# Two pairs of 512-column projections, from eight products to seven, in a two-layer encoder

## The chip, the core and the metric

The kernel is one program on one core of a Trainium2 chip. TensorE (PE) multiplies, VectorE (DVE), ScalarE (ACT) and GpSimd (POOL) do the elementwise work, and SyncE (SP) issues transfers. The metric is the device time of one execution in microseconds; lower is better.

## What is computed

Two layers on 512 tokens by 1024 channels, all float32. `u` is the RMS-normed input of a layer.

```python
proj = u @ w_in                                   # [512, 1024] @ [1024, 7424]
dq, dk, dv, rq, rk, rv, rg, gq, gk, gv, gates = split_cols(proj, IN_SPLITS)
a = differential_attention(rope(norm(dq)), rope(norm(dk)), dv, lam)      # 4 heads
r = silu(rg) * group_norm(bidirectional_retention(rope(rq), rope(rk), rv))  # 4 heads
c = grouped_query_attention(axial(norm(gq)), axial(norm(gk)), gv)        # 8 heads
merged = sum(sigmoid(gates) * (branches @ w_branch))                     # 3 branches
h = h + merged @ w_out
h = h + relu(rms_norm(h) @ w_mlp_in) ** 2 @ w_mlp_out
```

`c0` below means 256 columns of `dq` with 256 of `dk` (heads 0 and 1), `c1` the other 256 of each (heads 2 and 3).

## The kernel before

**Products.** TensorE's fast float32 (`fp32r`) takes a shortened number, so every operand is cut into a part `hi` and the rest `lo`. One product is then three matmuls: hi by hi, hi by lo, lo by hi. The weights come from memory in quarters of [128, 1024] through two `stage` buffers (SP's DMAs). ACT casts the quarter to `w_hi`, DVE subtracts it to give `w_lo` (line 417 records all of these operations, line 411 all matmuls). Six buffers hold the parts (`BUFS_W`).

**The mixing half of a layer** (`mix`) has a background and a side. The background (`bg`) is the stream of projections: `rv`; then for four heads `rq`, `rk`, `rg`; then `c0`, `dv`, `c1`, `gq`, each with tokens down the partitions (`units_b`: four token tiles, each of 8 k tiles by 3 matmuls of 512 columns); then `gkv`; then the merges of the three branches (`merge`), with gates and branch projections. The side is the attention: four retention heads (`ret_head`), four heads of the differential attention (`diff_head`), eight of the grouped one. `weave` puts `RATE` side steps beside each few passes of the background. A `diff_head` starts when all four token tiles of its `c` are there.

**Pairs in seven products.** Some gates (28 units in the program) and W1 of the MLP already use Winograd's form of Strassen's algorithm: two units of weights by two halves of tokens in seven products of half size in place of eight (`pair`). It needs sums of right operands; for the gates `turn_operands` makes them (lines with `xg`, `t`, `t23`, `t4`), in four steps within the merges (`TURN_AT`).

**What sets the order.** Every instruction is first noted (`Plan.note`), with a key in the order of the code. `Plan.order` then replays the program with a price for each instruction and lets each engine take the first ready one by key. What comes out is a fixed order for each engine: an engine that waits holds all that is behind it. So the diff shows little of how work moves, and the built order of each engine is shown with the change.

Buffers of [128, 512] come from one pool of 51 (`g`); PSUM has three banks for projections (`mm`), two for scores (`sc`), two for transposes (`tr`) and one for the sums of attention (`av`).

## Time and profile before

| | |
|---|---|
| runs shown | 1792.59 us median of 3, from 1791.82 to 1793.54 |
| span of the profiled execution | 1791.8 us, which is the time of the lowest run to 0.1 us |
| PE busy | 1767.7 us, 99% of the span, 10216 matmuls |
| DVE busy | 1376.4 us, 77% |
| ACT busy | 983.2 us, 55% |
| POOL busy | 297.1 us, 17% |
| granted TensorE clock | 1.000 (2.4 GHz) |
| transfers | 172.50 MB, 96 GB/s in the mean |

Busy shares are averages over stages. The record of a matmul or of a DVE operation is longer than the step to the next one, since the next begins before the last has drained: so what a stream of them costs is read from the starts in the timeline, not from the mean duration. `PE x <- DVE c` in the view of waits means that the matmul that writes `x` waited for the DVE operation that writes `c`.

### The profile page before, as it was taken

The numbers are of one execution on the slowest core, as the hardware profiler recorded it, in microseconds if no ns is written. First come the engines' busy times: TensorE is split into PE (matmuls) and PEld (weight loads), VectorE is DVE, ScalarE is ACT, GpSimd is POOL, SyncE is SP. The second block draws the span as 40 slices with busy tenths as digits, with TensorE's granted clock in tenths as the row PEclk, the third lists the DMA queues.
The fourth block names the chain that finished last, engine by engine and source line by source line (L and its number), as shares of the span: only waits on it lengthen the run. The fifth ranks groups of instructions, "written<-read, shape, count | busy, mean of one in ns | idle before, by whom it ended". The sixth has DMA issues, their size and how long they took to land.

```text
span 1791.8 us, 26264 instructions
## 1 busy us (share of the span) xinstructions
PE 1767.7 (99%) x10216; PEld 1544.8 (86%) x10216; DVE 1376.4 (77%) x2084; ACT 983.2 (55%) x1568; POOL 297.1 (17%) x294
## 2 busy tenths in 40 slices
PE   8999999999999999999999999999999999999999
PEld 6887888889989989999888778888888899989897
DVE  7866797899979766678656677968999797566783
ACT  5545666784446655445444455768844466444450
POOL 3334472002210000000013335700111100000000
PEclk9999999999999999999999999999999999999999
DMA  6311212112352323333432121121133423234331
GB/s 203 105 61 49 93 49 79 59 37 95 107 170 101 118 94 118 123 115 116 152 106 71 48 80 62 59 63 56 39 104 130 159 83 134 95 102 128 121 113 56
DMA packets 53691, 172.50 MB, mean 96 GB/s; under 512 B 6336, under 2 KB 6848, under 8 KB 53568
## 3 DMA queue, kind: packets, MB, share of 16 engines
q1 hardware_dynamic: 53568, 170.84, 29.4%
q8 instruction: 80, 1.31, 0.3%
q14 instruction: 43, 0.35, 0.1%
HBM read 162.43 MB, written 8.39 MB: 95 GB/s over the span
## 4 chain that ended last, share of the span: by engine, by line
PE 82%; DVE 8%; issue 3%; POOL 3%; ACT 2%; DMA 1%; SPq 0%; DVEq 0%; ACTq 0%; POOLq 0%
PE x L411 21%; PE w L411 20%; PE gate L411 6%; PE proj L411 5%; PE wo L411 5%; PE c L411 4%; PE wtr L413 2%; PE rv L411 2%; DVE w_lo L417 2%; PE rg L411 2%; PE rq L411 2%; PE dsc L411 2%; PE gav L411 2%; PE gsc L411 2%; DVE c L417 1%
## 5 line engine op out<-in xcount | busy, mean ns | idle before, releaser
L417 ACT CAST w_hi<-stage 128x1024 fp32r<-128x1024 f32 (+1 forms) x283 | 276.6, 982 | 319.7 <-PE w L411 120.7
L417 DVE TENSOR_TENSOR w_lo<-stage,w_hi 128x1024 fp32r<-128x1024 f32 (+1 forms) x283 | 336.9, 1192 | 78.7 <-ACT w_hi L417 75.8
L411 PE MATMUL x<-u,w_hi 128*128 128x256 f32 x1472 | 273.5, 284 | 5.3 <-DVE c L417 5.3
L411 PEld LDWEIGHTS x<-u,w_hi 128*128 128x128 f32 x1472 | 232.3, 192 | 10.9 <-DVE c L417 8.2
L411 PE MATMUL x<-u,w_lo 128*128 128x256 f32 x736 | 208.0, 283 | 0.0
L411 PE MATMUL w<-ml,w_hi 128*128 128x512 f32 (+1 forms) x520 | 200.3, 386 | 0.0
L411 PE MATMUL w<-mh,w_lo 128*128 128x512 f32 (+1 forms) x520 | 200.1, 386 | 0.0
L411 PE MATMUL w<-mh,w_hi 128*128 128x512 f32 (+1 forms) x520 | 200.1, 387 | 0.0
L411 PEld LDWEIGHTS x<-u,w_lo 128*128 128x128 f32 x736 | 141.1, 192 | 0.0
L417 ACT ACTIVATE c<-c 128x512 f32<-128x512 f32 x156 | 98.4, 631 | 32.9 <-DVE c L417 30.2
L411 PEld LDWEIGHTS w<-mh,w_lo 128*128 128x128 f32 x520 | 97.8, 188 | 19.5
L411 PEld LDWEIGHTS w<-ml,w_hi 128*128 128x128 f32 x520 | 97.8, 188 | 18.7
L411 PEld LDWEIGHTS w<-mh,w_hi 128*128 128x128 f32 x520 | 97.8, 188 | 18.5
L411 PE MATMUL gate<-u,w_hi 128*128 128x512 f32 x320 | 107.3, 399 | 0.0
L411 PE MATMUL x<-t23h,w_lo 128*128 128x256 f32 x368 | 104.2, 283 | 0.0
L411 PE MATMUL x<-t23l,w_hi 128*128 128x256 f32 x368 | 104.0, 283 | 0.0
L411 PE MATMUL x<-t23h,w_hi 128*128 128x256 f32 x368 | 103.9, 283 | 0.0
L417 ACT CAST w_hi<-sa 128x1024 fp32r<-128x1024 f32 x46 | 48.5, 1053 | 77.0 <-DVE sa L417 55.9
L411 PE MATMUL c<-w_hi,u 128*128 128x512 f32 x256 | 86.1, 394 | 0.0
L417 POOL TENSOR_TENSOR gth<-gth,c 128x512 f32<-128x512 f32 x28 | 45.9, 1647 | 179.0 <-DVE c L417 179.0
L417 DVE TENSOR_TENSOR c<-x,pu 128x512 f32<-128x512 f32 x92 | 63.1, 686 | 12.0 <-PE x L411 11.3
L411 PEld LDWEIGHTS x<-t23l,w_hi 128*128 128x128 f32 x368 | 70.6, 192 | 0.0
(278 smaller groups left out, 4554.5 us busy)
## 6 DMA issues: line engine op xcount, KB each, us to landing
stage<-in_w SPq DMA_DIRECT2D x283, 512.0 KB, 3.6
h<-in_x SPq DMA_DIRECT2D x16, 256.0 KB, 5.3
mid<-h SPq DMA_DIRECT2D x16, 256.0 KB, 2.0
h<-mid SPq DMA_DIRECT2D x16, 256.0 KB, 4.8
keep<-h SPq DMA_DIRECT2D x8, 256.0 KB, 4.1
h<-keep SPq DMA_DIRECT2D x8, 256.0 KB, 3.9
out<-h SPq DMA_DIRECT2D x7, 256.0 KB, 2.0
t_ret<-in_t_ret SPq DMA_DIRECT2D x4, 256.0 KB, 4.9
```

Of the source, the lines that this page charges most:

```text
L411: self.nc.tensor.matmul(k.pop("out"), **k)
L413: self.nc.tensor.transpose(k["out"], k["in_"], k["identity"])
L417: getattr(getattr(self.nc, o.engine), o.name)(**k)
```

## The change

`c0` with `dv`, and `c1` with `gq`, become two pairs in the seven-product form (`pair_wide`, keys `wa` and `wb`): A are 256-row halves of the two 512-column weights, B the token halves, and a product is [128 tokens, 512 columns] twice. Fourteen pieces of weights per pair are cut in place of eight quarters. The sums of weights (S1 to S4) are made by transfers: GpSimd issues a DMA that adds a quarter into the buffer `sa` or `sb`.

With it come: the right operands are made one step after each retention head, copied to memory and brought back in the merges, since they would fill the pool; the retention heads' results go to memory and back as well; `gkv` follows `rv`; `rq`, `rk`, `rg` of three heads and all branch weights are cut without DVE (`BY_DMA`): a GpSimd DMA casts to `w_hi`, ACT writes its negative to `w_lo`, a second GpSimd DMA adds the weight to it; prefetching goes by steps; `BUFS_W` is 5, `BUFS_G` 53, `RATE` 0.8; the Plan's price of a matmul is 11 ns higher.

```diff
+BY_DMA = {(nm, h) for nm in ("rq", "rk", "rg") for h in (1, 2, 3)} | {("br", n, i) for n in range(3) for i in range(4)}
+WIDE = ("A11", "A12", "S1", "S2", "S4", "S3", "A22")
+WIDE_PRODUCTS = (1, 2, 5, 6, 3, 7, 4)
-BUFS_W = 6
+BUFS_W = 5
-AHEAD_LOAD = 6
-AHEAD_SPLIT = 2
-BUFS_G = 51
-RATE = 1.0
+AHEAD = 2
+BUFS_G = 53
+RATE = 0.8
...
-            return 2.5 + n / 2.4 * (1 if n >= 256 else 4)
+            return 13.7 + n / 2.4 * (1 if n >= 256 else 4)
...
-        self.p_s = pool("s", 1)
+        self.p_s = pool("s", {"sa": 2, "sb": 1})
...
+    def cut_dma(self, q):
+        nc, n = self.nc, WIDTH[q % NQ]
+        hi, lo = (x[:, 0:n] for x in self.parts(self.p_w, 1024))
+        nc.gpsimd.dma_start(out=hi, in_=self.a["w"][q][:, 0:n])
+        nc.scalar.activation(out=lo, in_=hi, func=AF.Copy, scale=-1.0)
+        nc.gpsimd.dma_start(out=lo, in_=self.a["w"][q][:, 0:n], accum_op=ALU.add)
+        return hi, lo
...
+    def cut_wide(self, q, op, k):
...
+        if op[0] == "A":
+            return self.part(self.p_w, 1024, self.load(at(op)))
+        if op == "S1":
+            w[k] = self.load(at("A21"), self.p_s, "sa")
+        if op == "S3":
+            w[k] = self.load(at("A21"), self.p_s, "sb")
+        more(w[k], {"S1": "A22", "S2": "A11", "S3": "A11", "S4": "A12"}[op])
+        return self.part(self.p_w, 1024, w[k])
...
+    def pair_wide(self, l, key, u, n_cols, evs):
...
+        for o, n in enumerate(WIDE_PRODUCTS):
+            ps = [self.psum("mm", f"wide{n}")[:, 0:n_cols] for _ in range(2)]
+            for k in range(2):
...
+                for s in range(2):
+                    for j in (2 * k, 2 * k + 1):
+                        xh, xl = (self.right(u, n, p, j)[:, s * 128:(s + 1) * 128] for p in range(2))
+                        c = slice((j % 2) * n_cols, (j % 2 + 1) * n_cols)
+                        self.passes(ps[s], [(xh, hi[:, c]), (xh, lo[:, c]), (xl, hi[:, c])], j == 0, j == 3)
+                    yield
+            for s, p in enumerate(ps):
+                if n in (1, 5):
+                    copy(n, s, p)
+                elif n == 6:
+                    sub(kept[1, s], p, kept[1, s])
+                    sub(kept[5, s], kept[1, s], kept[5, s], ALU.add)
...
         def bg():
+            turn, uu = self.turn_operands(u), None
             yield from self.units_b(l, ("rv",), u, 512, 2, lambda p, t: self.ev_rv(p, t, st))
+            yield from self.units_b(l, ("gkv",), u, 256, 4, lambda p, t: self.ev_gkv(p, t, st))
             for h in range(4):
...
-            yield from self.units_b(l, ("c", 0), u, 512, 2, lambda p, t: self.ev_qk(p, 0, t, st))
-            yield from self.units_b(l, ("dv",), u, 512, 2, lambda p, t: self.ev_dv(p, t, st))
-            yield from self.units_b(l, ("c", 1), u, 512, 2, lambda p, t: self.ev_qk(p, 1, t, st))
-            turn, uu = self.turn_operands(u), None
+                uu = next(turn)
+            self.put_away(uu)
+            yield from self.pair_wide(l, ("wa",), uu, 512, [lambda x, t: self.ev_qk(x, 0, t, st),
+                                                            lambda x, t: self.ev_dv(x, t, st)])
+            back = self.bring_back(u)
...
-            yield from self.units_b(l, ("gq",), u, 512, 2, lambda p, t: self.ev_gq(p, t, st))
-            yield from self.units_b(l, ("gkv",), u, 256, 4, lambda p, t: self.ev_gkv(p, t, st))
-            yield from merge(1, True, False, "ret")
+            yield from merge(1, True, False, "ret", M1[0])
+            yield from self.pair_wide(l, ("wb",), uu, 512, [lambda x, t: self.ev_qk(x, 1, t, st),
+                                                            lambda x, t: self.ev_gq(x, t, st)])
+            yield ("after", "ret")
+            for h in range(4):
+                st["bT", 1, h] = (self.g("rTh", F32R), self.g("rTl", F32R))
+                for p, x in enumerate(st["bT", 1, h]):
+                    self.nc.sync.dma_start(out=x.bits(), in_=self.away["r", h, p])
+            yield from merge(1, True, False, "ret", M1[1])
```

**First place: DVE's queue where the heads of the differential attention meet the second projection of `q` and `k`.** (`qk<-c` and `qss` belong to the projection `c1`; `mx`, `drc`, `dE`, `dwl`, `dq` to differential heads; `w_lo` to cuts of weights.) Before, in `c1`:

```order
L417 TENSOR_TENSOR qk<-c,gqk 128x512
L417 RECIPROCAL drc<-dss 128x2
L417 TENSOR_REDUCE mx<-dsc 128x1
L417 TENSOR_TENSOR drc<-drc,lam 128x2
L417 TENSOR_REDUCE qss<-sq 128x8
L417 TENSOR_SCALAR qk_m<-qss,epst 128x8
L417 TENSOR_TENSOR dwl<-wtr,dwh 128x512
```

Now, in `wb` at its fourth product (`wide_2134` and `wide_2227` are that product's two PSUM banks, `p_...` the running sums in SBUF):

```order
L467 TENSOR_TENSOR w_lo<-sa,w_hi 128x1024
L467 TENSOR_TENSOR p_1994<-wide_2134,p_1994 128x512
L467 SCALAR_TENSOR_TENSOR dE_2141<-dE_2141,drc,dE_2178 128x512
L467 TENSOR_TENSOR p_2224<-p_1994,p_2224 128x512
L467 TENSOR_TENSOR w_lo<-sb,w_hi 128x1024
L467 TENSOR_TENSOR dwl<-wtr,dwh 128x512 x2
L467 TENSOR_TENSOR p_2001<-wide_2227,p_2001 128x512
L467 TENSOR_TENSOR w_lo<-stage,w_hi 128x1024
L467 TENSOR_TENSOR w_lo<-sa,w_hi 128x1024
L467 TENSOR_TENSOR dq<-qtr,dq 64x512 x2
```

The sums of the pair and the cuts of its pieces now stand between the steps of the heads.

**Second place: PE's queue in the same stretch.** (`u_...` are parts of x g; `t1h`, `t1l`, `t23h`, `t23l` parts of turned right operands; `dav` and `dsc` matmuls of a differential head.) Before, in `c1`:

```order
L411 MATMUL dav<-dwl,dvh 128x256
L411 MATMUL dav<-dwh,dvl 128x256
L411 MATMUL dav<-dwh,dvh 128x256
L411 MATMUL dav<-dwl,dvh 128x256
L411 MATMUL c<-w_hi,u_156 128x512
L411 MATMUL c<-w_lo,u_156 128x512
L411 MATMUL c<-w_hi,u_170 128x512
```

Now, at the change from the third product (`wide_2072`) to the fourth (`wide_2134`):

```order
L461 MATMUL wide_2072<-w_hi,t1h 128x512
L461 MATMUL wide_2072<-w_lo,t1h 128x512
L461 MATMUL wide_2072<-w_hi,t1l 128x512
L461 MATMUL wide_2134<-w_hi,t23h 128x512
L461 MATMUL dsc<-dkh,dq 128x512
L461 MATMUL dsc<-dkl,dq 128x512
L461 MATMUL wide_2134<-w_lo,t23h 128x512
L461 MATMUL wide_2134<-w_hi,t23l 128x512
```

A product's matmuls have the form of those of `c1`, three for each k tile, with the attention's between them; the left operands are turned ones.

**Third place: POOL's queue in the retention heads.** Before it held rotary work alone (`sw`, `rot`), the heads' factors (`msr`) and gates (`rx`):

```order
L417 TENSOR_TENSOR sw<-sw,t_ret 128x512
L417 TENSOR_TENSOR rot<-rot,sw 128x512
L417 TENSOR_TENSOR msr<-msq,mhalf 128x4
L417 TENSOR_TENSOR rx<-rx,rsg 128x512
L417 TENSOR_TENSOR sw<-sw,t_ret 128x512
```

Now the transfers that cast and add weights stand in it:

```order
L467 DMA w_hi<-in_w 128x1024
L467 DMA w_lo<-in_w 128x1024
L467 TENSOR_TENSOR msr<-msq,mhalf 128x4
L467 TENSOR_TENSOR sw<-sw,t_ret 128x512
L467 TENSOR_TENSOR rot<-rot,sw 128x512
L467 DMA w_lo<-in_w 128x1024
L467 DMA w_hi<-in_w 128x1024
L467 TENSOR_TENSOR rx<-rx,rsg 128x512
```

Each `w_lo` transfer waits for ACT, each `w_hi` transfer for PE to give back a buffer, and the rotary work behind them waits along.

## Rows read from the trace of the kernel before

**Rows 1.** The page, parts 1 and 2: busy time by engine; GB/s in 40 slices.

```profile
PE 1767.7 (99%) x10216; PEld 1544.8 (86%) x10216; DVE 1376.4 (77%) x2084; ACT 983.2 (55%) x1568; POOL 297.1 (17%) x294
...
GB/s 203 105 61 49 93 49 79 59 37 95 107 170 101 118 94 118 123 115 116 152 106 71 48 80 62 59 63 56 39 104 130 159 83 134 95 102 128 121 113 56
```

**Rows 2.** Busy time by stretch: mixing (180 to 300, 360 to 480), MLP (660 to 720).

```profile
core 0: us, PE busy (x) PEld busy (x) DVE busy (x) ACT busy (x) POOL busy (x), PEclk, DMA share, GB/s
180.00:240.00 60.00, 59.73 (x313) 48.99 (x312) 48.55 (x85) 37.90 (x73) 29.26 (x32) 1.00 0.21 66
240.00:300.00 60.00, 59.57 (x360) 51.77 (x359) 50.42 (x100) 39.61 (x80) 33.86 (x45) 1.00 0.24 82
360.00:420.00 60.00, 60.00 (x363) 52.74 (x363) 57.57 (x103) 45.07 (x84) 5.15 (x2) 1.00 0.17 52
420.00:480.00 60.00, 57.83 (x407) 53.72 (x406) 58.40 (x76) 26.23 (x34) 12.20 (x8) 1.00 0.29 99
660.00:720.00 60.00, 60.00 (x385) 54.81 (x384) 38.20 (x53) 29.41 (x40) 0.00 (x0) 1.00 0.33 106
```

**Rows 3.** Timeline of PE: start, duration, line, operation; 512, 256 and 128 columns.

```profile
699.81 0.39 PE L411 MATMUL w<-ml,w_hi 128*128 128x512 f32 x1
...
702.75 0.39 PE L411 MATMUL w<-mh,w_lo 128*128 128x512 f32 x1
...
252.11 0.28 PE L411 MATMUL dav<-dwh,dvl 128*128 128x256 f32 x1
252.23 0.28 PE L411 MATMUL dav<-dwh,dvh 128*128 128x256 f32 x1
...
183.73 1.03 PE L413 MATMUL wtr<-ident,dE 128*128 128x128 f32 x8
184.53 0.48 PE L411 MATMUL c<-w_hi,u 128*128 128x512 f32 x1
```

**Rows 4.** What PE waited for: us in total, times, longest.

```profile
PE x L411 <- DVE c L417: 5.3, 8, 0.9
...
PE dsc L411 <- ACT dkh L417: 1.6, 4, 0.5
PE qtr L413 <- POOL qk L417: 1.1, 2, 0.9
```

**Rows 5.** Timeline of DVE where it has no pause.

```profile
385.72 0.68 DVE L417 TENSOR_REDUCE mx<-gsc 128x1 f32<-128x512 f32 x1
386.32 0.68 DVE L417 TENSOR_TENSOR t23l<-t,t23h 128x512 fp32r<-128x512 f32 x1
386.92 0.68 DVE L417 TENSOR_REDUCE mx<-gsc 128x1 f32<-128x512 f32 x1
...
388.19 1.20 DVE L417 TENSOR_TENSOR w_lo<-sb,w_hi 128x1024 fp32r<-128x1024 f32 x1
389.31 0.15 DVE L417 RECIPROCAL grc<-gss 128x1 f32<-128x1 f32 x1
389.38 0.67 DVE L417 TENSOR_REDUCE mx<-gsc 128x1 f32<-128x512 f32 x1
```

**Rows 6.** Groups of DVE from 120 to 440 us: count, busy us, mean ns.

```profile
L417 DVE TENSOR_TENSOR w_lo<-stage,w_hi 128x1024 fp32r<-128x1024 f32 x35 | 46.4, 1330 | 3.3 <-ACT w_hi L417 3.0
L417 DVE SCALAR_TENSOR_TENSOR dE<-dE,drc,dE 128x512 f32<-128x512 f32 x16 | 12.8, 798 | 0.9 <-ACT dE L417 0.8
```

**Rows 7.** Groups of ACT, POOL and DVE over the whole program.

```profile
L417 ACT CAST w_hi<-stage 128x1024 fp32r<-128x1024 f32 (+1 forms) x283 | 276.6, 982 | 319.7 <-PE w L411 120.7 <-DMA stage<-in_w 80.2 <-PE x L411 62.2
L417 POOL TENSOR_TENSOR qk_r<-qk_m,mhalf 128x8 f32<-128x8 f32 x16 | 29.4, 1840 | 103.0 <-ACT dkh L417 64.3 <-DVE qk_m L417 28.0 <-DVE drc L417 10.6
L417 DVE TENSOR_SCALAR decay<-delta,dec 128x896 f32<-128x896 f32 x8 | 6.0, 751 | 0.4 <-DMA delta<-in_delta 0.2
```

**Rows 8.** DMA issues: count, KB each, median us from issue to landing.

```profile
stage<-in_w SPq DMA_DIRECT2D x283, 512.0 KB, 3.6
...
delta<-in_delta SPq DMA_DIRECT2D x2, 448.0 KB, 5.5
```

**Rows 9.** The tile `w_lo`: durations in ns, least, median, most.

```profile
L417 DVE TENSOR_TENSOR w_lo<-stage,w_hi x283: 676/1224/2361, 10.9 to 1755.9; 128x1024 fp32r<-128x1024 f32 x110, 128x512 fp32r<-128x512 f32 x32
```

More of the change, by code (lines that the diff above doesn't have):

```diff
@@ L93, in gate, with merge @@
         a_unit(("gate", n, i), "w_in", cols(GATE + n * D + i * 128, 128))
-    def merge(n):
-        for i in range(8):
+    def merge(n, its=range(0, 8, 2)):
+        for i in [j for k in its for j in (k, k + 1)]:
             gate(n, i)
@@ L120, with steps @@
 NQ = len(PLAN)
+WIDTH = [len(r) // 128 * len(c) for _, _, r, c in PLAN]
 PAIRED = {WIDX["w1", f] for f in range(0, 32, 2)} | {WIDX["gate", n, i] for n in GATE_PAIRS for i in range(GATE_PAIRS[n], 8, 2)}
+def steps():
+    out, at, q = [], {}, 0
+    while q < NQ:
+        key = PLAN[q][0]
+        at[key] = len(out)
+        if key[0] in ("wa", "wb"):
+            at[key[:1]] = len(out)
+            out += [("wide", q, op, k) for op in WIDE for k in range(2)]
+            q += 8
+        elif q in PAIRED:
+            out.append(("pair", q))
+            q += 2
+        else:
+            out.append(("dma" if key in BY_DMA else "one", q))
+            q += 1
+    return out, at
+WIDE = ("A11", "A12", "S1", "S2", "S4", "S3", "A22")
+WIDE_PRODUCTS = (1, 2, 5, 6, 3, 7, 4)
+STEPS, STEP_AT = steps()
+NS = len(STEPS)
 BUFS_STAGE = 2
-BUFS_W = 6
+BUFS_W = 5
 BUFS_WH = 2
 BUFS_MID = 3
-AHEAD_LOAD = 6
-AHEAD_SPLIT = 2
-BUFS_G = 51
-RATE = 1.0
+AHEAD = 2
+BUFS_G = 53
+RATE = 0.8
 HOP = 200.0
@@ L242 @@
 class Op:
-    __slots__ = ("engine", "name", "args", "kwargs", "key", "cost", "deps", "tiles", "new", "left", "outs", "end",
-                 "ready")
+    __slots__ = ("engine", "name", "args", "kwargs", "key", "cost", "late", "deps", "tiles", "new", "left", "outs",
+                 "end", "ready")
 class Plan:
@@ L295, in note @@
         o.cost = price(engine, name, kwargs) if engine != "sync" else self.dma_price(kwargs)
+        o.late = self.LATENCY.get(engine, 0.0)
+        if engine == "gpsimd" and name == "dma_start":
+            o.cost, o.late = (880.0, 5600.0) if "accum_op" in kwargs else (600.0, 3800.0)
         self.ops.append(o)
@@ L397, in order @@
                 result.append(pick)
-                heapq.heappush(events, (now + o.cost + self.LATENCY.get(e, 0.0), 0, pick))
+                heapq.heappush(events, (now + o.cost + o.late, 0, pick))
                 heapq.heappush(events, (busy[e], 2, pick))
@@ L458, in __init__ @@
         nc.sync.dma_start(out=self.gains, in_=a["gains"])
-        self.loaded = self.cut = 0
-        self.stage, self.w = {}, {}
+        self.cut = 0
+        self.w, self.wide = {}, {}
+        self.away = {}
     def tables(self):
@@ L969, in ret_head @@
         self.split(x, hi, lo)
-        st["bT", 1, h] = (hi, lo)
+        for p, x in enumerate((hi, lo)):
+            nc.sync.dma_start(out=self.away["r", h, p], in_=x.bits())
         yield ("pe", 2)
@@ L1096, in gqa_head @@
         nc = self.nc
-        yield ("need", ("gkv", 3))
+        yield ("need", ("gq", 3))
         if kv == 0:
```

180 lines of the change are left out of this document (116 added, 64 removed).

## The prediction

> **What bounds the kernel now.** I read the busy shares first. PE is busy for 99% of the span, DVE for 77%, ACT for 55%, POOL for 17% [rows 1]. These are averages over stages, so I read the stretches next: while the projections and the attention run (180 to 300 us) PE is busy 59.6 to 59.7 of every 60 us and DVE 48.6 to 50.4; in the MLP PE is busy for 60.00 and DVE for 38.2 [rows 2]. The granted clock is 1.00 in all of them. A busy PE could still be one that waits inside its records, so the third view is the timeline of PE. From 699.81 to 702.75 us lie 13 steps of 512 columns, 0.226 us each, though each record lasts 0.39; 256 columns step by 0.12, and eight transposes need 0.80, so 0.10 each [rows 3]. These steps, multiplied by the counts of the program, fill the span but for some 40 us. So PE's queue of matmuls is the bound nearly everywhere, and a matmul less is worth its step. The waits say the same from the other side: the largest inside the program are 5.3 us of `x` on DVE, 1.6 of `dsc` on ACT, 1.1 of `qtr` on POOL [rows 4].
>
> **The change part by part.**
>
> *Matmuls removed.* A projection of 512 columns takes 4 token tiles x 8 k tiles x 3 = 96 matmuls of 512 columns, two of them 192. The pair takes 7 products x 2 x 4 x 3 = 168 of the same width. That is 24 less for a pair, 96 less for two pairs in two layers. At 0.226 us [rows 3] this is 21.7 us. No other matmul is added: the built program has 10138 before and 10042 now.
>
> *DVE in the pairs.* A pair adds 14 sums of 512 columns on DVE, and 14 cuts in place of 8. What counts is the stretch in which this falls. I counted both queues of the changed kernel from the first matmul of `wb` to the first branch projection. PE has 224 matmuls of 512 columns, 48 of 256, 56 transposes and 4 of one column: 50.6 + 5.8 + 5.6 + 0.4 = 62.4 us. DVE has 15 cuts, 66 operations over 512 columns, 12 with a scalar per row (`dE` and the like) and 24 small ones. A record over 512 columns lasts 0.68 us, but the next one starts after 0.60; a cut lasts 1.20, and the next operation starts after 1.12; a small one steps by 0.07 [rows 5]. Cuts are slower while POOL runs, 1.33 in the mean [rows 6], so I take 1.2 as their step, 0.70 for the 0.80 us of `dE` [rows 6] and 0.12 for the small ones, which wait a little on each other. That is 18.0 + 39.6 + 8.4 + 2.9 = 68.9 us. DVE then needs 6.5 us more than PE in this stretch, 13.0 in two layers. Before, the same stages left DVE idle for 10 us of every 60 [rows 2]. The ends: where PE can run ahead of DVE through the whole stretch, it costs 0, as from 360 to 420 us, where DVE is busy 57.6 of 60 and PE 60.00 [rows 2]. Where records instead of steps decide (1.27 for a cut, 0.68, 0.78, 0.2), DVE needs 78 us, 15 more than PE, 30 in two layers. I take 13.0, since the steps are read where DVE has no pause, and this is such a place. In `wa` the same count gives PE 43 us and DVE 35, so no cost.
>
> *What that swallows.* PE's 1.6 + 1.1 us of waits on `dkh` and `qk` [rows 4] lie in these stages. If DVE sets their length, they are inside it: -2.7 us.
>
> *Turned operands and branch cuts leave the merges.* Made in the retention heads now, the operands take about 15 us of DVE steps a layer out of the merges (8 sums of 512, 16 of 256, six splits), and the 12 branch weights that are cut by transfers another 12 x 1.12 [rows 5] = 13. There DVE is busy for 57.6 to 58.4 of 60 and PE waits 5.3 us for it [rows 2, 4]. I take half of that wait, -2.6; ends 0 and -5.3. In the heads DVE gets the 15 us but loses nine cuts, 10 us; from the first `rq` to `wa` the same count gives PE 86 us and DVE 61, so nothing is added.
>
> *Weights cut by transfers.* 42 pieces: 84 GpSimd DMAs and 42 passes of ACT, which take the place of its casts of 0.98 us [rows 7]. The chain is cast landing, ACT, sum landing: 3.6 + 1.0 + 3.6 = 8.2 us, if these transfers land as SP's of the same size do [rows 8]; at 5.5, the slowest load of about this size [rows 8], it is 12.0. Against it stands the PE work between the point where a buffer is given back and the piece's first use, counted from the built order with the steps above: 17 us and more for most, 14.7 for one piece a layer, 11.3 for one. I take 0; the ends are 0 and +2. DVE's two-input operations and POOL already slow each other: the cut lasts 1.22 us in the median and up to 2.36 [rows 9].
> The Trainium skill (SBUF — State Buffer, section Who interferes with whom) speaks against such transfers: it says that descriptors of a GpSimd DMA cannot be written while DVE holds the shared port pair, which its two-port modes do for a whole operation and `tensor_tensor` does not. No run here shows such a DMA yet. By that rule the cuts block nothing, and only the decay tables' `tensor_scalar`, 8 x 0.75 us [rows 7], would; as an estimate this adds at most 6.0 us to the sum, 1784.6.
>
> *Copies to memory and back.* 48 pieces of 256 KB go out and 48 come in, on SP, whose queue otherwise waits for stage buffers. With the GpSimd transfers the traffic rises by some 68 MB to about 135 GB/s in the mean; single slices reach 170 and 203 already [rows 1]. Cost 0: the pieces are needed a merge later. If that cover goes, a late piece holds SP's weight loads behind it by one landing, 3.6 us [rows 8], eight times at most.
>
> *The rest.* `gkv` moves forward with the same work. Five buffers for weights in place of six shorten the lead of a cut in the MLP from 21 to 17 us of PE work in the median; a cut needs 1.0 + 1.1, so 0.
>
> *Sum.* The profiled execution's span is 1791.8 us: 1791.8 - 21.7 + 13.0 - 2.7 - 2.6 = 1777.8. The median of the runs stands 0.8 above that span, so the forecast is **1778.6 us**, its own range 1770 to 1787.
>
> **The rivals.**
>
> *DVE's overhang hides.* PE and DVE share no tight buffer for long enough, and PE runs ahead: no 13.0, so 1765.6. For it: the stretch from 360 us. Against it: there the order had not been filled beyond DVE's capacity; here DVE's queue is longer than PE's.
>
> *The chain of sums of weights.* S1, S2 and S4 are made in one buffer, each by a transfer that must wait for the cut of the one before. A link is a POOL operation in front (up to 1.84 [rows 7]), a landing of 3.6, a cast of 0.98 and a cut of 1.12: 5.7 to 7.5 us. PE gives a link 24 matmuls, 5.4 us, where no attention lies between, as in most of `wa`. Two links in each of four pairs, 0.3 to 2.1 us each if no lead is left, and 2 more each if an adding transfer takes so much longer than a load: 3 to 33 us, so 1781 to 1811. I put its middle low, at 10 us and 1789, since the first sum of a pair can be made before the pair begins and only `wa` lacks work between.
>
> *ACT held by landings: slower.* ACT takes its work in order, and 42 of its passes wait for a `w_hi` transfer. If one lands 1.9 us later than the order was made for (5.5 in place of 3.6 [rows 8]), ACT stands still for 80 us in all, with the softmax behind it; it is busy for 38 to 45 of 60 [rows 2], so I let a third reach PE: +26.6, 1805. It decides from (1796.2 - 1778.6) / 42 = 0.42 us of PE per piece.
>
> *DVE at record lengths.* +30 in place of +13: 1796, no change.
>
> **How the numbers follow.** A measurement here tells some 0.2%, 3.6 us, from no change. Chances: the forecast 0.46, the hidden overhang 0.17, the chain of sums 0.20, ACT held 0.10, record lengths 0.07. Faster takes the first two and half of the third: 0.73. No change takes the last and 0.07 of the third: 0.14. Slower takes the rest: 0.13. The range must reach the hidden overhang below, 1765, and most of the chain of sums above, 1794; what is left out is the slower case and the edges.
>
> **What would show it.** Right: 96 matmuls fewer at a step of 0.226 us; DVE busy above 57 of 60 us in `wb` in both layers and PE's waits there on DVE (`p`, `w_lo`, `dkl`); waits of `x` on `c` in the merges below 5.3 us; GpSimd's transfers landing within 4 to 6 us with no wait of PE on their `w_lo`. Wrong: PE waiting for `w_hi` or `w_lo` of `sa` or `sb` (chain of sums), ACT idle before `w_lo` on a DMA with PE idle behind it (held), or a step of the wide matmuls above 0.23 us.

## The result, and the profile after

The changed kernel takes 1856.4 us in the median of four runs (1856.05 to 1858.51), the kernel before 1792.2 (1791.79 to 1793.54). The ratio is 1.036 (1.034 to 1.037): slower by 64 us, where 13.6 us less had been forecast. The profiled execution of the changed kernel took 1856.76 us, its span 1855.0.

The page of the changed kernel, part 1, the row of the granted clock and the chain that ended last; it answers to [rows 1]:

```profile
PE 1778.1 (96%) x10120; PEld 1535.0 (83%) x10120; DVE 1399.5 (75%) x2118; ACT 1014.1 (55%) x1604; POOL 394.3 (21%) x410
...
PEclk9999899999999999999999999999999999999999
...
PE 67%; DVE 14%; ACT 7%; DMA 4%; issue 4%; POOL 4%; ACTq 0%; SPq 0%; POOLq 0%; DVEq 0%
```

PE has 96 matmuls less and yet is busy for 10 us longer. It is busy for 96% of the span, no longer for 99%, and POOL's time has grown by 97 us. The same stretches as in [rows 2]:

```profile
core 0: us, PE busy (x) PEld busy (x) DVE busy (x) ACT busy (x) POOL busy (x), PEclk, DMA share, GB/s
180.00:240.00 60.00, 49.70 (x222) 38.58 (x221) 48.57 (x74) 33.02 (x56) 31.23 (x35) 0.91 0.62 138
240.00:300.00 60.00, 53.72 (x263) 40.91 (x262) 59.42 (x95) 39.92 (x77) 43.05 (x41) 1.00 0.50 139
360.00:420.00 60.00, 59.86 (x354) 51.94 (x353) 48.08 (x83) 42.90 (x79) 5.89 (x7) 1.00 0.48 140
420.00:480.00 60.00, 58.32 (x410) 53.23 (x409) 51.62 (x80) 39.87 (x71) 12.21 (x11) 1.00 0.37 96
660.00:720.00 60.00, 60.00 (x393) 55.10 (x391) 38.87 (x54) 30.90 (x44) 0.00 (x0) 1.00 0.31 104
```

The MLP (last row) is as it was. From 240 to 300 us DVE has no room left (59.42 of 60). In `wb` itself, from 205 to 268 us, it is busy for 61.81 of 63 us, as forecast. From 180 to 240 us, where `wa` ends, PE stands still for 10 us and DVE isn't full: something else holds them. What PE waited for, answering to [rows 4] (`rsc` are the scores of a retention head, `rkh` one of their operands):

```profile
PE wide L461 <- ACT w_hi L467: 17.3, 2, 8.8
PE x L461 <- DVE c L467: 7.3, 4, 2.2
PE rsc L461 <- ACT rkh L467: 7.2, 4, 4.3
PE rv L461 <- ACT w_hi L467: 7.2, 1, 7.2
PE ms L461 <- ACT gsq L467: 6.5, 6, 3.2
PE ms L461 <- DVE dq L467: 3.9, 4, 1.7
PE dsc L461 <- ACT dE L467: 3.1, 4, 1.3
```

The list is long and flat, and it names ACT where it named DVE before. Its first row is one wait a layer, for the second half of S3. The timeline of PE around it in the first layer (start, duration, operation, in brackets the idle time before):

```profile
186.97 0.39 PE L461 MATMUL wide<-w_hi,t4l 128*128 128x512 f32 x1
187.20 0.40 PE L461 MATMUL wide<-w_hi,t4h 128*128 128x512 f32 x1
196.16 1.22 PE L461 MATMUL wide<-w_hi,t23h 128*128 128x512 f32 x2 [8.56 <-ACT w_hi L467]
...
197.60 0.63 PE L461 MATMUL wide<-w_hi,t4l 128*128 128x512 f32 x1
198.03 0.63 PE L461 MATMUL wide<-w_hi,t4h 128*128 128x512 f32 x1
```

Before the wait a wide matmul steps by 0.23 us, as in [rows 3]; behind it by 0.43. The stretches of 4 us there show why:

```profile
184.00:188.00 4.00, 3.60 (x18) 2.64 (x16) 3.36 (x6) 1.68 (x3) 2.62 (x5) 1.00 0.86 203
188.00:192.00 4.00, 0.00 (x0) 0.00 (x0) 0.17 (x1) 0.00 (x0) 3.33 (x4) 0.83 1.03 228
192.00:196.00 4.00, 0.00 (x0) 0.00 (x0) 0.00 (x0) 0.94 (x1) 0.00 (x0) 0.50 1.03 252
196.00:200.00 4.00, 3.85 (x9) 3.07 (x10) 3.10 (x4) 1.05 (x2) 0.69 (x1) 0.50 0.46 138
200.00:204.00 4.00, 4.00 (x15) 2.90 (x15) 2.85 (x5) 1.69 (x3) 4.00 (x7) 0.89 0.49 145
```

While PE stands still the granted clock falls from 1.00 (2.4 GHz) to 0.50 (1.2 GHz), and PE works at half speed for some 4 us after. The DMA engines are busy all the time there (the view gives a share of 1.03). What ACT waited for, and the longest transfers in the chain that ended last (start, duration), tell what the stall is made of:

```profile
ACT w_lo L467 <- DMA w_hi<-in_w: 30.0, 15, 6.3
...
ACT w_hi L467 <- DMA sb<-in_w: 17.2, 2, 8.8
```

```profile
59.00 7.87 DMA w_hi<-in_w
95.75 8.43 DMA w_hi<-in_w
184.17 10.79 DMA sb<-in_w
```

The adding transfer of S3 that was issued at 184.17 us landed 10.79 us later, with two other adding transfers and two loads under way; ACT stood for it, and PE for ACT. A cast issued at 59.00 us landed after 7.87 us; ACT did the `w_lo` that waited for it and only then `rkh`, for which PE had been waiting 4.3 us. The DMA issues of the weights, with median landings, answering to [rows 8]:

```profile
stage<-in_w SPq DMA_DIRECT2D x233, 512.0 KB, 3.6
w_hi<-in_w POOLq DMA_DIRECT2D x42, 512.0 KB, 4.3
w_lo<-in_w POOLq DMA_DIRECT2D x42, 512.0 KB, 5.7
sa<-in_w POOLq DMA_DIRECT2D x24, 512.0 KB, 6.1
...
sb<-in_w POOLq DMA_DIRECT2D x8, 512.0 KB, 6.5
```

So the saving is there, and more than that is lost. I counted the loss by stage from the timeline of PE: the length of a stage less its operations at their steps (0.227 us for 512 columns, 0.12 for 256, 0.11 for a transpose). The steps of the program add up to 1750 us before and 1727 after; what remains between the first and the last matmul is 30 us before and 116 after. So 86 us of new loss stand against a saving of 22. In the table both layers are added up; "half clock" is PE's busy time in stretches of 4 us times what the granted clock lacks of 1.00, and is part of the loss. The rows below the first two are experiments, told in the next section. Each row comes from one profiled execution.

```
PE's loss, us          heads  wa, wb or   to the last  to the last  to   half
                              c0 to gkv   diff score   gqa score    wo   clock
before                   5.2     10.9        -0.2          3.4      7.4    0
after                   28.4     38.7        18.5         11.7     12.5   13.6
e1 no weight DMA        19.7     35.6        16.9         17.5      6.5   11.9
e3 no sums S            28.5     29.2        16.3         11.3     11.0   14.8
e4 no product sums      26.2     28.7        26.9         13.0     12.5   19.2
e5 = e1 and e3          17.4     28.7        12.8         16.7      6.9    8.0
e8 = e5, no rotations   17.7     22.6         6.4         16.7      6.9    4.7
e10 = e5, not turned     7.2     29.5        12.2         13.0      6.9   11.1
e12 all of these         6.2      9.9         6.2         13.0      5.7    1.6
e14 = e12, old order     6.2     11.0         4.2          6.9      3.3    1.7
e11 before + DMA        10.3     14.9        -0.4         10.6      8.0    7.9
e18 before, new order    6.2     14.3         0.8         21.4      2.8    3.0
```

No stage of the mixing is spared, and no single one holds the loss.

### The profile page after: what moved, and what is told of

Its sections match the earlier page's. It is cut to its first block, busy times and chain, and to the rows that moved or that the text cites. A ratio compares the mean times of both kernels' runs of the same rounds, so it can differ in the third digit from the quotient of the medians.

```text
span 1855.0 us, 26501 instructions
## 1 busy us (share of the span) xinstructions
PE 1778.1 (96%) x10120; PEld 1535.0 (83%) x10120; DVE 1399.5 (75%) x2118; ACT 1014.1 (55%) x1604; POOL 394.3 (21%) x410
## 4 chain that ended last, share of the span: by engine, by line
PE 67%; DVE 14%; ACT 7%; DMA 4%; issue 4%; POOL 4%; ACTq 0%; SPq 0%; POOLq 0%; DVEq 0%
PE x L461 20%; PE w L461 19%; PE wo L461 5%; PE gate L461 4%; PE proj L461 4%; PE wide L461 4%; DVE w_lo L467 3%; DMA w_hi<-in_w 2%; PE rv L461 2%; ACT w_hi L467 2%; PE wtr L463 2%; PE gsc L461 1%; DVE mx L467 1%; DMA stage<-in_w 1%; DMA sb<-in_w 1%
## 5 line engine op out<-in xcount | busy, mean ns | idle before, releaser
L467 ACT CAST w_hi<-stage 128x1024 fp32r<-128x1024 f32 (+1 forms) x233 | 224.6, 964 | 300.4 <-PE w L461 114.3
L467 DVE TENSOR_TENSOR w_lo<-stage,w_hi 128x1024 fp32r<-128x1024 f32 (+1 forms) x233 | 273.1, 1175 | 87.1 <-ACT w_hi L467 85.9
L467 DVE TENSOR_TENSOR w_lo<-sa,w_hi 128x1024 fp32r<-128x1024 f32 x70 | 88.6, 1266 | 18.5 <-ACT w_hi L467 14.4
L467 ACT CAST w_hi<-sa 128x1024 fp32r<-128x1024 f32 x70 | 73.5, 1050 | 51.9 <-PE w L461 25.3
L467 POOL DMA_DIRECT2D sa<-in_w x24 | 23.1, 960 | 363.8 <-DVE decay L467 321.1
L467 DVE TENSOR_TENSOR w_lo<-sb,w_hi 128x1024 fp32r<-128x1024 f32 x54 | 66.4, 1230 | 32.4 <-ACT w_hi L467 32.2
L467 ACT CAST w_hi<-sb 128x1024 fp32r<-128x1024 f32 x54 | 56.7, 1051 | 55.7 <-PE x L461 21.0
L461 PE MATMUL x<-t23h,w_lo 128*128 128x256 f32 x256 | 72.6, 284 | 0.0
L461 PE MATMUL x<-t23h,w_hi 128*128 128x256 f32 x256 | 72.4, 283 | 0.0
L461 PE MATMUL x<-t23l,w_hi 128*128 128x256 f32 x256 | 72.4, 283 | 0.0
```

What stands on the lines that cost most here:

```text
L461: self.nc.tensor.matmul(k.pop("out"), **k)
L467: getattr(getattr(self.nc, o.engine), o.name)(**k)
```

## The experiments

One caution covers all: the Plan makes a new order for every kernel, so a difference is the price of the edit together with the order that it brings. How much an order can be worth is measured below (e9, e18). The kernel before took 1791.8 to 1792.6 us in the median beside each group of runs.

### Four parts, each by itself

**e1**, the weight pieces cut as before:

```diff
-BY_DMA = {(nm, h) for nm in ("rq", "rk", "rg") for h in (1, 2, 3)} | {("br", n, i) for n in range(3) for i in range(4)}
+BY_DMA = set()
```

> The 42 weight pieces that GpSimd's transfers cut are cut as before, by ACT and DVE; the sums S1 to S4 are still transfers. Transfers theory (ACT, which takes its work in order, is held by late w_hi, and the transfers crowd each other): the losses outside the two waits on S3 go for the most part; PE's loss against its steps falls from 116 us to 60-80 and the time from 1856 to 1805-1825, although DVE gets 42 cuts of 1.12 us, 47 us, more. DVE theory (the sums of products and the cuts bound it): the 47 us of cuts lengthen it, 1856-1885. Sums theory (only the single buffer of S3 counts): no more than 5 us off, 1850-1860.

Measured: 1844.7 us (1843.2 to 1848.3), 11.7 below the changed kernel, though DVE is busy for 40 us more. The loss in the heads falls from 28.4 to 19.7. The sign is that of the transfers theory, which had 31 to 51 us: the size is a quarter to two fifths of that.

**e2**, a second buffer for S3:

```diff
-            w[k] = self.load(at("A21"), self.p_s, "sb")
+            w[k] = self.load(at("A21"), self.p_s, ("sb", "sa")[k])
```

> The second half of S3 is built in a buffer of sa, so that it needn't wait for the cut of the first half. Sums theory: the waits of 8.8 us of the wide matmuls on w_hi, one a layer, go, and the stretch at half clock behind each with them (4 us each): 25 us off, 1830. Transfers theory: the other landings stay late; 8 to 15 us off, 1841-1848. DVE theory: 0 to 5 us off.

Measured: 1856.0 us (1852.1 to 1859.1), no difference. That is the range of the DVE theory alone, though the edit doesn't touch DVE. The longest wait of `wide` on `w_hi` falls from 8.8 to 6.5 us and others grow. In the changed kernel the wait in the first layer ended with a landing of 10.79 us, so the buffer alone didn't set its length.

**e3**, no sums of weights:

```diff
-        more(w[k], {"S1": "A22", "S2": "A11", "S3": "A11", "S4": "A12"}[op])
-        return self.part(self.p_w, 1024, w[k])
+        return self.part(self.p_w, 1024, self.load(at({"S1": "A22", "S2": "A11", "S3": "A21", "S4": "A12"}[op])))
```

> The sums of weights S1 to S4 are left out: each is a plain load of one quarter by SP, so that no transfer adds and no chain of three sums lies in one buffer. What the kernel computes in c0, dv, c1 and gq is then another product. Sums theory: all of the losses in wa and wb that are not DVE's go: 30 to 45 us off, 1811-1826. Transfers theory: 42 casts and 42 adds remain: 10-20 us off, 1836-1846. DVE theory: 0 to 5 us off.

Measured: 1844.0 us (1840.2 to 1845.6), 12.4 less, where the sums theory had 30 to 45 and the transfers theory 10 to 20. PE's waits for `w_hi` in the pairs are gone, and one that was 1.0 us in all is now among the larger ones:

```profile
PE wide L461 <- DVE w_lo L467: 5.2, 4, 2.1
```

PE reaches `wb` earlier and meets DVE there. From the first matmul of the pairs to their middle the loss fell from 12.3 to 1.5 us in the first layer; in the second half it rose from 7.1 to 13.2.

**e4**, ten of 14 sums of products:

```diff
                 elif n == 6:
-                    sub(kept[1, s], p, kept[1, s])
-                    sub(kept[5, s], kept[1, s], kept[5, s], ALU.add)
+                    pass
                 elif n == 7:
-                    x = kept.pop((5, s))
-                    sub(x, x, p)
-                    ended(1, 1, s, x)
-                    sub(kept[1, s], kept[1, s], p)
+                    ended(1, 1, s, kept.pop((5, s)))
                 elif n == 4:
-                    x = kept.pop((1, s))
-                    sub(x, x, p, ALU.add)
-                    ended(1, 0, s, x)
+                    ended(1, 0, s, kept[1, s])
```

> Ten of the 14 sums of products on DVE in each pair are left out: products 6, 7 and 4 are made and not added, and their columns are the ones of products 1 and 5 alone. DVE has 10 x 0.60 = 6.0 us less work in each of four pairs. DVE theory: wb no longer needs more of DVE than of PE, and 13 us and what hangs on them go: 13 to 30 us off, 1826-1843. Transfers theory and sums theory: the landings hold PE as before, 0 to 8 us off, 1848-1856.

Measured: 1857.2 us (1855.1 to 1861.2), no difference, with DVE busy for 24 us less. This speaks against my own account of `wb`, by DVE's count of operations, though not wholly: in the table the loss in the pairs falls by 10.0 us, and 8.4 come back in the stage behind them. What became of the time is seen in the groups of DVE from 200 to 300 us. The first block is the changed kernel, the second e4, the third the kernel before (count, busy us, mean ns):

```profile
L467 DVE TENSOR_TENSOR w_lo<-stage,w_hi 128x1024 fp32r<-128x1024 f32 x9 | 11.7, 1311 | 0.0
...
L467 DVE TENSOR_TENSOR p<-p,gq_r 128x512 f32<-128x512 f32 x4 | 5.1, 1269 | 0.0
```

```profile
L467 DVE TENSOR_TENSOR w_lo<-stage,w_hi 128x1024 fp32r<-128x1024 f32 x9 | 18.0, 2000 | 5.1 <-ACT w_hi L467 4.9
```

```profile
L417 DVE TENSOR_TENSOR gqx<-gq,gq_r 128x512 f32<-128x512 f32 x4 | 2.7, 684 | 0.0
```

A cut that takes 1.31 us in the mean takes 2.00 in e4. The product with `gq_r`, which read PSUM before and reads two SBUF tiles in the pair, takes 1.27 us in place of 0.68. POOL is busy for 43 of 60 us there, where it was for 34 [rows 2]. So DVE's length in `wb` is made by what runs beside it as well as by its count. The traces show this record by record. In the changed kernel 255 of the 311 cuts of 1024 columns lie beside no elementwise operation of POOL, and none of them takes longer than 1.23 us; every longer one, up to 2.77, lies beside one. In e4 one of the nine took 5.01 us, beside five POOL operations in a row. The sums `p<-wide,p`, which read one operand from PSUM, take 0.68 to 0.69 us beside POOL and without it.

### Two at a time, and one pair at a time

**e5** has the edits of e1 and e3 together.

> No transfer by GpSimd at all: the 42 pieces are cut by ACT and DVE (as in e1) and the sums S1 to S4 are left out, each a plain load (as in e3). If the two costs are separate, 11.6 and 12.3 us add up: 1856.4 - 24 = 1832. DVE and POOL theory (the stretch of wb from 210 to 300 us is set by DVE, slowed by POOL's operations, so that what is saved ahead of it is lost again in it): 1836-1845, with PE's loss in wb and the start of the merges above the 15 us a layer of the changed kernel. Transfers theory alone (nothing else new): about 1775.

Measured: 1831.8 us (1830.2 to 1834.7), 24.6 less; 11.7 and 12.4 add up to 24.1. So the two prices of transfers add.

**e6** and **e7** take back one pair each. The edit of e6 is shown; e7 does the same with `c0` and `dv`:

```diff
-            yield from self.pair_wide(l, ("wb",), uu, 512, [lambda x, t: self.ev_qk(x, 1, t, st),
-                                                            lambda x, t: self.ev_gq(x, t, st)])
+            yield from self.units_b(l, ("c", 1), u, 512, 2, lambda p, t: self.ev_qk(p, 1, t, st))
+            yield from self.units_b(l, ("gq",), u, 512, 2, lambda p, t: self.ev_gq(p, t, st))
```

> Only wa stays a pair; c1 and gq are projected by token tiles as before, all else as in the changed kernel. PE gets 24 x 2 = 48 matmuls, 10.9 us, back. DVE and POOL theory: most of the 15 us a layer that PE loses in wb and the first 40 us of the merges goes: 1856.4 + 10.9 - 20 to 30 = 1837-1847. Transfers theory: the sums of wb go with it, but those of wa and the 42 pieces stay: 1862-1867.

> Only wb stays a pair; c0 and dv are projected by token tiles as before, all else as in the changed kernel. PE gets 10.9 us back. Sums theory: PE's loss in wa falls from 12.3 to 3 us a layer: 1856.4 + 10.9 - 19 = 1848, or less where wb's sums now have a longer lead. DVE and POOL theory: wb and the merges lose 28 us a layer as they do now, and the 19 us of wa come back there in part: 1850-1860.

Measured: 1856.6 us (1853.4 to 1862.9) without the pair `wb`, 1851.6 (1848.6 to 1856.7) without `wa`. Either pair costs about what its 48 matmuls save, or somewhat more: `wb` 10.9 us, `wa` about 5 us beyond that. e6 lies between its two expectations; e7 is in the range of the DVE and POOL theory and 4 us above that of the sums theory, so the two tell little apart.

**e8** is e5 without the rotations of `c0`, `c1` and `gq`:

```diff
-            nc.gpsimd.tensor_tensor(out=y[:, :, o:o + 8], in0=x3[:, :, 8 - o:16 - o],
...
-        self.axial(x, 8, "q", t, x)
```

> As e5, and POOL's rotations of c0, c1 and gq are left out (the operations over token tiles behind the pairs; those of the retention heads and of gk stay), so the queries and keys of those heads aren't rotated. DVE and POOL theory: DVE is no longer slowed from 210 to 300 us and the softmax's operands come sooner; 20 to 30 us below e5. DVE's count theory (its own operations fill the stretch): 0 to 5 us below e5. Merges theory (the loss lies in their end, from 420 to 550 us, and comes from the copies brought back): 0 to 3 us below e5.

Measured: 1818.1 us (1816.5 to 1819.3), 13.7 below e5: between the 20 to 30 of the DVE and POOL theory and the 0 to 5 of the others. The groups of DVE from 200 to 300 us, e5 first, then e8:

```profile
L467 DVE SCALAR_TENSOR_TENSOR dE<-dE,drc,dE 128x512 f32<-128x512 f32 x12 | 10.7, 895 | 0.0
L467 DVE TENSOR_TENSOR p<-p,gq_r 128x512 f32<-128x512 f32 x4 | 3.3, 814 | 1.0 <-POOL gq_r L467 1.0
```

```profile
L467 DVE SCALAR_TENSOR_TENSOR dE<-dE,drc,dE 128x512 f32<-128x512 f32 x12 | 8.9, 742 | 0.0
L467 DVE TENSOR_TENSOR p<-p,gq_r 128x512 f32<-128x512 f32 x4 | 2.7, 684 | 0.3 <-POOL gq_r L467 0.3
```

The same operations are shorter once POOL does less: 895 to 742 ns, 814 to 684. The whole loss from the first projection to the last score of the differential heads falls from 41.5 to 29.0 us. The rotations also stand on the way to `qtr`, the transposes of the queries, so the run doesn't part what DVE loses by them from what their own length costs.

### The order, the operands, and the transfers in the kernel before

**e9** sets two numbers of the order back:

```diff
-RATE = 0.8
+RATE = 1.0
-            return 13.7 + n / 2.4 * (1 if n >= 256 else 4)
+            return 2.5 + n / 2.4 * (1 if n >= 256 else 4)
```

> The changed kernel with the two numbers of the order as they were: RATE 1.0 in place of 0.8 (attention steps per step of a projection) and 2.5 in place of 13.7 ns in the planner's price of a matmul; nothing else. Order theory (the attention runs 55 us later against the gates than before, 354 to 492 us in place of 298 to 399, because of these numbers): 1825-1845. Theory that the pair itself delivers its columns late, and the other costs: within 8 us of 1856.

Measured: 1864.9 us (1859.1 to 1868.3), 8.5 slower, which neither theory had. With everything else in place the new numbers are the better ones.

**e10** is e5 without the turned operands and their copies:

```diff
-            turn, uu = self.turn_operands(u), None
+            half = lambda j: (u[0][j], u[1][j])
+            uu = {"u": u, "v": [half(j) for j in range(4)], "w": [half(4), half(5)], "t1": [half(6), half(7)]}
...
-                uu = next(turn)
-            self.put_away(uu)
```

> As e5 (1831.8), and the operands of the pairs are not made: where they stood, the normalised input itself is read, so that the 24 sums and six splits a layer, their 16 buffers and their copies to memory and back are left out, and what the pairs compute is another product. Heads theory (e5 loses 8.0 and 4.2 us more in the heads than the kernel before, DVE having up to 27.7 of 30 us of work there; the turning does it): 10 to 15 us below e5, 1817-1822, with PE's loss in the heads at 2 to 5 us a layer. Copies theory: also 3 to 6 us less in the merges, 1811-1818. Rival (the loss comes from the order of the heads): 1828-1834.

Measured: 1816.0 us (1813.6 to 1818.2), 15.8 below e5, a little more than the heads theory had and within the range of the copies theory. The loss in the heads falls from 17.4 to 7.2 us, near the 5.2 of the kernel before; in the merges (last three stages) from 36.4 to 32.1. Turning and copying weren't parted.

**e11** puts the 42 transfers into the kernel before, with the changed kernel's prices of such issues in the Plan. The part that cuts a piece:

```diff
+            if t is None:
+                nc.gpsimd.dma_start(out=hi, in_=self.a["w"][q])
+                nc.scalar.activation(out=lo, in_=hi, func=AF.Copy, scale=-1.0)
+                nc.gpsimd.dma_start(out=lo, in_=self.a["w"][q], accum_op=ALU.add)
```

> The kernel before, with the 9 pieces of the heads and the 12 of the branches cut by GpSimd's transfers as in the changed kernel; no pairs of 512 columns, no sums of weights. Transfers theory (ACT is held by late landings whatever else is there): e1 got 6.6 and 3.8 us back in the heads, so 1792 + 8 to 14 = 1800-1806. Rival (the transfers are harmless where no sums and no copies use the engines of the DMA at the same time, and DVE has 47 us less work): 1786-1793.

Measured: 1812.5 us (1810.4 to 1815.7), 19.9 slower than the kernel before, more than any theory had, with DVE busy for 53 us less. What PE waited for in this kernel, then ACT and POOL:

```profile
PE rsc L415 <- ACT rkh L421: 6.0, 2, 3.6
...
PE dav L415 <- DVE dwl L421: 3.4, 1, 3.4
```

```profile
ACT w_lo L421 <- DMA w_hi<-in_w: 24.3, 14, 5.5
```

```profile
POOL w_hi L421 <- PE gate L415: 151.2, 8, 30.6
POOL w_lo L421 <- ACT w_lo L421: 133.9, 29, 9.4
```

None of PE's larger waits is for a transferred piece itself. ACT stands still 14 times until `w_hi` has landed, with `rkh` and the softmax behind it in its queue; and POOL's queue stands for up to 30.6 us before an issue, until PE has given a buffer back, with its other work behind. PE's two longest single waits, but for the one at the program's start, can be followed back in the trace. The one of 3.6 us for `rkh` ends a chain in which a cast landed 7.48 us after its issue and ACT did `w_lo` before `rkh`. The one of 3.4 us for `dwl` follows a cut on DVE that took 5.38 us in place of 1.2, beside nine operations of POOL in a row:

```profile
282.90 5.38 DVE L421 TENSOR_TENSOR w_lo<-stage,w_hi 128x1024 fp32r<-128x1024 f32 x1 [1.01 <-ACT w_hi L421]
```

**e12** leaves out what e4, e5, e8 and e10 leave out.

> What e4, e5, e8 and e10 leave out, all of it: no GpSimd transfers, no sums of weights, ten of 14 sums of products, no rotations behind the pairs, no turned operands and no copies of them. What stays of the change is its 96 matmuls less, 24 more pieces to cut, and that a pair gives its columns late. If the causes named so far make up the loss: 1770-1785 (the kernel before less 21.8 us is 1770). If the late columns and the order cost by themselves: 1790-1810.

Measured: 1788.7 us (1787.1 to 1792.5; ratio to the kernel before 0.998, 0.997 to 0.999). That lies between the two expectations. It is 43.1 below e5, where e8 and e10 account for 13.7 and 15.8. The remaining 13.6 came with the product sums, which were worth nothing in e4. That their cost is hidden while something else holds PE would fit, but no run puts the sums alone back into e12, and the order changed too, so this is not shown. The time is still 18.3 above the kernel before less 96 matmuls (1792.2 - 21.8 = 1770.4).

### What was left open: ACT's wait, and the order

**e13** and **e15** free ACT from the landings, in the kernel before and in the changed one:

```diff
-                nc.scalar.activation(out=lo, in_=hi, func=AF.Copy, scale=-1.0)
+                nc.scalar.activation(out=lo.rearrange("p (a b) -> p a b", a=2), in_=self.other.unsqueeze(1).to_broadcast([128, 2, 512]),
+                             func=AF.Copy, scale=-1.0)
```

> As e11 (the kernel before with 42 pieces cut by transfers, 1812.5), but ACT's pass reads another resident tile of the same size in place of the w_hi that has just been sent for, so that ACT waits for no landing; the transfers, their sizes and ACT's work stay, and the lower parts of these weights are other numbers. ACT theory: most of the 20 us go, 1793-1800. Crowding theory (the transfers land late for PE, or slow the loads beside them): 1808-1813.

> The changed kernel with the edit of e13: ACT's passes for the 42 pieces read another resident tile and wait for no landing; all transfers stay. ACT theory: the 12 us that e1 gained, and more, since DVE is spared its 42 cuts: 1836-1846. Crowding theory: 1852-1858.

Measured: e13 1807.3 us (1807.0 to 1808.0), 5.2 below e11; e15 1847.6 (1844.1 to 1851.3), 8.9 below the changed kernel; each lies between the ranges of its two theories. ACT's wait is a quarter of the 19.9 us; in e13 the loss at half clock goes with it (7.9 to 1.5 us). The other 14.7 us aren't settled: later landings, POOL's queue, DVE beside POOL and the order are left, and no run parts them.

**e14** is e12 with the two numbers of e9.

> As e12 (1788.7), with the two numbers of the order as before (RATE 1.0, 2.5 ns), so that the attention runs earlier against the gates. If its later place costs the 18.6 us that e12 lies above 1770: 1772-1782. If the late columns of a pair cost them wherever the attention is put: 1786-1796.

Measured: 1778.3 us (1778.0 to 1778.7), 10.4 below e12. In e12 the scores of the grouped heads run until 458 us and in e14 until 430; PE's loss up to there falls from 13.0 to 6.9. The expectation of a later place was right here, and wrong in e9. e14 computes less than the changed kernel, so its 13.4 us below the kernel before are no gain of the whole computation.

**e18** gives the kernel before the numbers of the changed one.

> The kernel before with the two numbers of the order of the changed kernel (RATE 0.8, 13.7 ns). If the later place of the attention costs by itself, as e14 against e12 has it (10 us): 1798-1804. If the numbers only matter together with the pairs: 1790-1795.

Measured: 1813.5 us (1812.6 to 1814.1), 21.4 slower. This was expected by none of the theories at this size. The stretch that was full before [rows 2] loses the most of PE's busy time:

```profile
360.00:420.00 60.00, 56.60 (x326) 48.88 (x325) 48.42 (x88) 38.01 (x70) 10.27 (x2) 0.97 0.17 52
```

```profile
PE x L411 <- ACT pu L417: 6.0, 2, 3.0
```

PE was busy for 60.00 us and DVE for 57.57; now it is 56.60 and 48.42. Of the 3.4 us that PE stands still there, 3.0 are one wait for `pu`, a copy on ACT in the first pair of gates, and the clock falls behind it; the kernel before has no such wait in its list. The scores last until 443 us in place of 399, and the rest of the loss is spread over many short waits.

### The whole computation, repaired

**e16** and **e17** keep one pair or both, cut all weights on ACT and DVE, make the sums of weights on DVE and set the two numbers back:

```diff
-        more(w[k], {"S1": "A22", "S2": "A11", "S3": "A11", "S4": "A12"}[op])
+        t = self.load(at({"S1": "A22", "S2": "A11", "S3": "A11", "S4": "A12"}[op]))
+        nc.vector.tensor_tensor(out=w[k], in0=w[k], in1=t, op=ALU.add)
```

> The whole computation: only wa is a pair, c1 and gq by token tiles; no GpSimd transfers, the sums of weights are made by DVE (8 of 1024 columns a layer, about 9 us), RATE and the planner's price as before. The pair saves 24 matmuls a layer, 10.9 us in all: 1781 if nothing is lost. The heads lose 4 to 6 us a layer for the turned operands (e5 against e10): 1789-1795 if that is all. If DVE's work behind wa (sums, cuts, sums of weights) reaches PE too: 1796-1810.

> The whole computation with both pairs: no GpSimd transfers, the sums of weights by DVE, RATE and the planner's price as before. From e5 (1831.8): the sums of weights on DVE cost 8 x 1.1 us a pair where DVE is full in wb, up to 18 us in all; the order's numbers between -10 (e14) and +8.5 (e9): 1822-1858, likeliest 1840. Below 1812 would mean that the transfers alone were the loss.

Measured: 1807.4 us with `wa` alone (1805.0 to 1808.8; ratio to the kernel before 1.008, 1.006 to 1.010), 1853.5 with both (1852.6 to 1853.6). The first is in the highest of its three ranges, the second at the upper end of its one. No version with the whole computation comes below the kernel before. With both pairs PE loses 53.2 us in the stages of `wa` and `wb` alone: the work that the transfers took from DVE is back on DVE, which is busy for 74.73 of 80 us in `wb`, and PE's largest wait in the mixing is for DVE's `dE` (9.9 us in all).

## Why the prediction was wrong

The forecast was 1778.6, the result 1856.4. The sum failed at what it put at nothing: the weights cut by transfers (0; 11.7 to 19.9 us in the runs), the operands made in the heads (0; 15.8), and the order with its two new numbers (no term; 8 to 21 us in either direction). The sums of weights, which it kept as a rival, cost 12.4 on top. Term by term:

- **Matmuls removed, -21.7: right.** The wide step is 0.23 us at the full clock, and the program's steps add up to 22 us less.
- **Weights cut by transfers, 0 with ends 0 and +2: the step that failed first.** By themselves they cost the kernel before 19.9 us (e11), and taking them out of the changed kernel gives 11.7 (e1). I compared a piece's own chain (8.2 to 12.0 us) with the PE work until its use, and that comparison holds: PE hardly waits for these pieces. What I left out is who stands in the queue behind a piece: ACT's other passes and POOL's other operations. The rival "ACT held" had the mechanism, and its sign, at a chance of 0.10; I priced it at 26.6 us and its part is 5.2 (e13) to 8.9 (e15). The landings I took from SP's transfers, 3.6 us with 5.5 as the slow end; they are 4.3 for a cast and 5.7 for an adding one in the median, and the casts that held ACT in the chain that ended last took 7.87 and 8.43. The Plan of the changed kernel itself sets 3.8 and 5.6 us for these landings, in lines that I passed over. The 6.0 us that the prediction worked out beside the sum from the Trainium skill (SBUF — State Buffer, section Who interferes with whom), for issues that DVE holds up, don't show: the longest record of such an issue in the changed kernel is 1.53 us, the medians 0.60 to 0.91.
- **The chain of sums, a rival at 0.20 with 3 to 33 us, middle 10: its size was right.** e3 gives 12.4. The place was not: the long stall is at S3, not along S1, S2 and S4, and a second buffer there gives nothing (e2). The forecast itself had no term for it, and that is the fault: I set the rivals against each other, where transfers of weights, sums and the full DVE all held at the same time, and 11.7 and 12.4 simply add.
- **DVE in `wb`, +13.0: right in its place, wrong in its reason.** DVE is full there (61.81 of 63 us, and 61.95 of 63 in the second layer), and PE loses 7.1 us in the second half of the pairs of the first layer, where 6.5 had been forecast. But that the sizes agree is partly luck: 24 us less of DVE's work alone moved a part of the loss behind the pairs and left the time as it was (e4), while POOL's rotations, which are no work of DVE's, are worth 13.7 (e8). I read the steps of a DVE that has no pause [rows 5], and knew that a cut lasts up to 2.36 us beside POOL [rows 9]; I didn't ask which operations of the pair read two SBUF tiles where they had read PSUM. The Trainium skill (SBUF — State Buffer, section Who interferes with whom) says that a DVE instruction with two SBUF inputs contends with a GpSimd instruction that reads SBUF. The rows agree: the product with `gq_r` takes 0.68 us from PSUM before, 1.27 from SBUF now, and 0.68 again in e8 with the rotations left out.
- **What that swallows, -2.7: right by the letter.** The waits for `dkh` and for POOL's `qk` are gone from PE's list, but others of the differential heads came in their place: 3.1 us of `dsc` on `dE`, and 3.9 of `ms` on `dq`.
- **Operands made in the heads, "nothing is added": wrong.** They cost 15.8 us (e10, copies included); PE's loss in the heads falls by 10.2 without them. I compared PE's 86 us with DVE's 61 over the whole stretch. An average over heads hides what one head's chain through ACT, DVE and POOL waits for; which link of it is late was not parted.
- **The merges relieved, -2.6: wrong.** `x` waits 7.3 us for `c`, not 2.7.
- **The rest: a term that was missing.** The diff showed `RATE` and a higher price of a matmul, and I gave them no term. On the kernel before they cost 21.4 us by themselves (e18); in the changed kernel setting them back costs 8.5 (e9); with the other parts out it gives 10.4 (e14). A number that sets an order has no price of its own: it fits one mixture of work and not another.
- **Half clock: no term either.** The granted clock was 1.00 throughout before [rows 2], and I took that as given. Behind stalls of 8.56 and 4.3 us it was 0.50, and the loss at the lower clock is 13.6 of the 86 us.
- **Copies, five buffers:** not tried by themselves.

From the changed kernel the runs lead down by 24.6 us for all GpSimd transfers (e5), 43.1 for operands, rotations and product sums together (e12), 10.4 for the order (e14), which ends at 1778.3. That this is so near the forecast of 1778.6 is chance: the forecast had 13.0 us for DVE in it, and e14 leaves most of that work out. The 7.9 us from there to 1770.4 stay open, and so does the split of the transfers' 14.7 us behind e13. Since an order alone can be worth 8 to 21 us, these prices are those of an edit and its order together.

## What to carry to other kernels

Where PE is at 99%, a saved matmul is worth its step, but every edit that pays for it with another queue must be priced also by what stands behind it in that queue (here ACT's and POOL's), not only by the lead of the piece that it brings. Costs that can hold at the same time can't be set as alternatives: the transfers of weights and the sums added up (e5), and a cost can look like nothing by itself (e4) and still be part of what is found when several are left out together (e12). Where a sum moves an operand from PSUM to SBUF, ask what POOL does beside the operation that reads it. An order that was fitted to one mixture of work is a term of its own; change its numbers alone, on the old kernel and on the new, before its gain or loss is put down to anything else.

## What the runs showed of the hardware

- In the changed kernel, after 8.56 us without a matmul, PE ran at 0.43 us per 512 columns in place of 0.23 for some 4 us, with a granted clock of 0.50. A stall of 4.3 us in the heads (`rsc` on `rkh`) was followed by the same: 0.50 from 68 to 72 us.
- A GpSimd transfer of 512 KB that casts landed 4.3 us after its issue in the median, one that adds 5.7 to 6.5, beside 3.6 for a plain load by SP. The Trainium skill (DMA: Bandwidth & Descriptors, section Anatomy of one DMA — SWDGE (gpsimd) path) fits a GpSimd transfer by 2.0 us plus one us for each 436 KB, which gives 3.2 us for this size as an estimate: the trace has it a third longer for a cast and 1.8 to 2 times as long for an adding one. Beside other transfers, at a DMA share of 1.03, one that adds took 10.79 us.
- DVE's operations with both inputs in SBUF grew beside POOL by more than I had allowed. No cut of 1024 columns in any run took longer than 1.23 us without an elementwise operation of POOL beside it; beside POOL one took 5.66 us (e4). `dE` took 0.895 us in the mean in e5 and 0.742 in e8, which has less for POOL to do. An operation with one input in PSUM (`p<-wide,p`) took 0.68 to 0.69 us in the changed kernel either way.
